# Normalised input of token blocks 2 to 8: half-precision pairs kept in DRAM and read back transposed by DMA, in place of transpositions on TensorE

## The chip, the cores and the metric

The kernel runs on one core of a Trainium2 chip. Its engines, each with its own in-order queue of instructions, are TensorE (PE in the profile, with PEld for its weight loads), VectorE (DVE), ScalarE (ACT), GpSimd (POOL) and SyncE (SP); SP and GpSimd also issue DMAs. The metric is the device time of one launch in microseconds, smaller being better; where several runs are given it is their median.

## The reference

A two-layer decoder trunk on 2048 tokens of width 1024: a Mamba-2 mixer, then multi-head latent attention (MLA), each behind an RMS norm with gain, with residual adds.

```python
def rms_norm(x, g):
    y = xf * lax.rsqrt(jnp.mean(xf * xf, axis=-1, keepdims=True) + EPS)
    return y * g
# layer 1: Mamba-2
hn = rms_norm(x, g_pre[0])
proj = hn @ w_in                      # gate z, conv input xBC, dt: 1024 -> 5152
xBC = silu(causal_depthwise_conv(xBC, conv_w, conv_b))
y = ssd_chunked_scan(xh, softplus(dt + bias), A, B, C) + D_skip * xh
h = x + group_norm(y * silu(z)) * g_out @ w_out
# layer 2: MLA
ckv, k_rope = split(rms_norm(h, kv_g_in) @ w_dkv);  k_nope, v = rms_norm(ckv) @ w_ukv
cq, gate = split(rms_norm(h, g_pre[1]) @ w_in);     q = rms_norm(cq) @ w_uq
h = h + (causal_attention(q, k, v) * silu(gate)) @ w_out
out = rms_norm(h, g_final)
```

The result has single precision. The kernel gets near it with half-precision products by splitting every factor into a pair, `hi` (rounded to half precision) and `lo` (the remainder), and adding three products, hi*hi + hi*lo + lo*hi.

## The kernel before

**Blocks.** The tokens are worked in blocks of 512 (`TB`). There are eight of them in the sense of this document: blocks 1 to 4 are the four quarters of the sequence as input of the Mamba layer, blocks 5 to 8 the same quarters of `h` as input of the MLA layer's projections. (In the code they are `xT[0]` to `xT[7]`.) After them come attention and the output projection, which the change doesn't touch.

**The input of a block.** Every product with the normalised input needs it with channels on the partitions: eight tiles `xT` of [128 channels, 2 halves of the pair, 512 tokens] in half precision, in eight buffers that the next block takes over one by one. `load_x` loads four tiles of 128 rows by 1024 channels (`hx`; for one block `hs`), squares them on ScalarE, makes reciprocal roots on VectorE (`rows_rms`, `rsqrt`: 12 small operations) and scales the rows (line 574). `prep` then makes the eight tiles: for each of eight groups of 128 channels four transpositions on TensorE into one PSUM bank (`transposed`, line 262), and from there the pair (`pair16`): ScalarE writes `hi` (line 115), VectorE the remainder `lo` (line 116). In the Mamba layer the pair's scale is the gain `g0` of the channel, in the MLA layer a constant, since the MLA weights hold their gain.

**Mamba.** The work runs over 16 items (block, group of heads). While the state scan `ssd` of an item is done in 20 pieces, the queue of TensorE gets beside it the output projection `outp` of the item before, and the input products `xbc` and the gate's `zgate` of the next item. `sweep` orders the products of these: channel groups 0 and 1 for all four banks, then 2 to 5 group by group, then 6 and 7 bank by bank. In the third item of a block, `load_x` of the next block is called, and `prep` is spread under the last `zgate` of the block, which is the last user of the old `xT`. Behind it stands `steps` (step sizes dt of the next block, 16 products with `wdt`, line 729), which needs all eight new tiles.

**Weights.** In block 1 the weights come raw (`wraw`, or held tiles), are split in `wpair` into pairs (`wsp`) with the scale `up` of their kind, and are kept in DRAM (`wi_d`, written by `settle`); later blocks load them from there. `scan` and `powers` find these scales. The output weights are handled likewise in blocks 1 and 2 (`w_out`, `wo_d`). Weight loads are written with a raised priority.

**MLA.** For each of four blocks: `load_x` of the next block, `mla_kv_down` and `mla_cq` (products with one `xT` tile after another), the upper projections `mla_up` beside the gate's products `mla_gate`, and under the second half of `mla_gate` (the last user of `xT`) the `prep` of the next block.

**Order.** Nothing is placed by hand: a scheduler puts the instructions on the engines' queues by their priority and a model of their times, and gives each its waits. Nearly all DMAs are issued on SP's one queue, where a DMA that waits holds up those behind it.

Of the kernel before, what the change touches and what calls it, by code (L numbers as in the profile page):

```python
# [12 lines left out]
BF16 = mybir.dt.bfloat16  # L13
# [54 lines left out]
class Net:  # L68
# [93 lines left out]
    def scan(self, g, kinds, place, hold=False, early=0):  # L162
# [40 lines left out]
    def wpair(self, b, kind, g, k, w):  # L203
# [4 lines left out]
        with self.tc.high_priority(AHEAD):  # L208
            u = self.t(self.wp, "wsp", [P, 2, 2, n], F16, bufs=WSP)
            d = self.wi_d[kind][g, k // 2]  # L210
            if b == 0:
# [9 lines left out]
                for j, raw in enumerate(raws):  # L221
                    self.pair16(u[:, j, 0], u[:, j, 1], raw, self.up[:, g, kind:kind + 1])
# [54 lines left out]
    def layer_constants(self, cp):  # L277
# [14 lines left out]
        self.up, self.down = (cp.tile([P, G, 3], F32, name=n) for n in ("up", "down"))  # L292
        self.half = cp.tile([P, G], F32, name="half")
# [19 lines left out]
        nc.vector.tensor_scalar(self.g0, self.g0, up[:, 0:1], 1.0 / 32, ALU.mult, ALU.mult)  # L313
        self.pair16(self.wdt[:, :, 0], self.wdt[:, :, 1], wdt.rearrange("p (k c) -> p k c", k=KD), up[:, 1:2])
# [21 lines left out]
    def mamba(self, cp):  # L336
# [32 lines left out]
        for part in (hold, self.prep(0, self.g0), rest[0], self.steps(0), together(self.xbc(0, 0), rest[1]),  # L369
# [10 lines left out]
        for n, (b, g) in enumerate(items):  # L380
# [4 lines left out]
            turned = iter(())  # L385
            if g == G - 2:
                self.load_x(b + 1, self.a["x"][(b + 1) * TB:(b + 2) * TB] if b + 1 < NB else self.h_d[0:TB])
                turned = behind(self.prep(b + 1, self.g0 if b + 1 < NB else None, each=1), 2)
            if n + 1 < len(items):
# [7 lines left out]
                parts += [beneath(self.xbc(*items[n + 1]), beside), beneath(self.zgate(*items[n + 1]), beside, turned)]  # L397
# [162 lines left out]
    def load_x(self, b, src, tag="hx"):  # L560

        nc = self.nc
        self.xn[b] = xs = [self.t(self.hh, tag, [P, D], bufs=4) for _ in range(4)]
# [3 lines left out]
        parts = 4 if b == 0 else 1  # L567
        for c in range(parts):
            for i, x in enumerate(xs):
                v = x[:, c * D // parts:(c + 1) * D // parts]  # L570
                if parts > 1 and i == 3:
# [4 lines left out]
    def prep(self, b, gain=None, tag="tr", each=4):  # L576
# [3 lines left out]
        for k in range(KD):  # L580
            ps = self.transposed(xs, k, tag)
            u = self.t(self.xq, "xT", [P, 2, TB], F16, bufs=8)
            self.pair16(u[:, 0, :], u[:, 1, :], ps, XSCALE if gain is None else gain[:, k:k + 1])
            self.xT[b].append(u)
            if k % each == each - 1:
                yield

# [343 lines left out]
    def mla(self, early):  # L931
# [5 lines left out]
        for b in range(NB):  # L937
            last = b == NB - 1
            if not last:
# [705 lines left out]
```

## Time and profile before

| | |
|---|---|
| runs | 2917.16 us median of 3 (2916.06 to 2920.21) |
| profiled execution | 2911.01 us, span 2909.2 us |
| mean granted TensorE clock | 0.993 |
| block boundaries in the Mamba layer (`steps` begins) | 356.6, 723.1, 1088.0 us |
| Mamba layer and MLA projections end about | 2000 us |
| ScalarE, GpSimd busy | 1828.1 us (63%), 860.4 us (30%) |
| DMA | 441.40 MB, 152 GB/s mean |

"Busy" counts the time in which an engine has an instruction in work; products on TensorE overlap, so the distance between two starts, and not the length of one, is what it costs. In the grouped views a row has the code line, engine, operation, output <- input (buffer numbers left out), shape, count, and then busy time, mean ns of one, idle time before the group and what ended it. In a timeline the columns are start, length, engine, line, operation, names, count, and in brackets the idle time before it.

### The profile page before, as it was taken

The numbers are of one execution on the slowest core, as the hardware profiler recorded it, in microseconds if no ns is written. First come the engines' busy times: TensorE is split into PE (matmuls) and PEld (weight loads), VectorE is DVE, ScalarE is ACT, GpSimd is POOL, SyncE is SP. The second block draws the span as 40 slices with busy tenths as digits, with TensorE's granted clock in tenths as the row PEclk, the third lists the DMA queues.
The fourth block names the chain that finished last, engine by engine and source line by source line (L and its number), as shares of the span: only waits on it lengthen the run. The fifth ranks groups of instructions, "written<-read, shape, count | busy, mean of one in ns | idle before, by whom it ended". The sixth has DMA issues, their size and how long they took to land.

```text
span 2909.2 us, 58684 instructions
## 1 busy us (share of the span) xinstructions
PE 2833.6 (97%) x21582; PEld 1668.1 (57%) x21582; DVE 2109.2 (73%) x5068; ACT 1828.1 (63%) x3976; POOL 860.4 (30%) x984
## 2 busy tenths in 40 slices
PE   7899999999999999999999999999999999999998
PEld 3465566555555554554555545555666666665787
DVE  6789887787777778779775554456777777778454
ACT  8777756666566766556553433334888888888522
POOL 0222221221221212222211121213665666665300
PEclk9999999999999999999999999999999999999999
DMA  8755536444464446635445655662212222222453
GB/s 286 256 191 190 177 121 207 150 144 153 160 233 132 152 136 229 220 118 192 157 147 204 206 183 176 204 196 81 67 52 67 67 53 72 64 67 88 169 194 109
DMA packets 244899, 441.40 MB, mean 152 GB/s; under 512 B 69890, under 2 KB 111650, under 8 KB 243172
## 3 DMA queue, kind: packets, MB, share of 16 engines
q1 hardware_dynamic: 233476, 401.74, 43.0%
q0 software_dynamic: 11136, 35.92, 3.4%
q8 instruction: 169, 2.77, 0.4%
q14 instruction: 118, 0.97, 0.1%
HBM read 332.83 MB, written 104.73 MB: 150 GB/s over the span
## 4 chain that ended last, share of the span: by engine, by line
PE 43%; issue 3%; DVE 3%; ACT 2%; DMA 1%; POOL 1%; DVEq 0%; SPq 0%; POOLq 0%; ACTq 0%
PE s L1326 4%; PE s L1327 4%; PE mm L84 4%; PE s L1328 4%; PE mm L86 4%; PE mm L85 4%; PE s L1213 4%; PE tr L84 3%; PE tr L86 3%; PE tr L85 3%; PE o L1366 2%; PE o L1367 2%; PE o L1365 2%; DVE junk L1215 1%; PE s L1394 0%
## 5 line engine op out<-in xcount | busy, mean ns | idle before, releaser
L1350 POOL TENSOR_TENSOR PTs<-x,PTs 128x512 f16<-128x512 f32 (+1 forms) x380 | 439.0, 1178 | 263.5 <-ACT PTs L1337 174.5
L1332 ACT ACTIVATE x<-s 128x512 f32<-128x512 f32 (+3 forms) x640 | 326.7, 524 | 50.3 <-PE s L1328 31.6
L84 PE MATMUL mm<-xT,wsp 128*128 128x512 f16 x800 | 306.6, 383 | 7.9 <-ACT wsp L115 5.6
L85 PE MATMUL mm<-xT,wsp 128*128 128x512 f16 x800 | 306.1, 383 | 0.0
L86 PE MATMUL mm<-xT,wsp 128*128 128x512 f16 x800 | 305.3, 382 | 0.0
L1337 ACT ACTIVATE PTs<-x 128x1024 f16<-128x1024 f32 (+1 forms) x320 | 297.2, 929 | 9.4
L1215 DVE CUSTOM_DVE_ANT_0 junk<-s,fence,mx 128x512 bf16<-128x512 f32 (+1 forms) x372 | 242.1, 651 | 43.7 <-PE s L1213 3.0
L1367 PE MATMUL o<-K,PTs 128*128 128x65 f16 x2176 | 262.2, 192 | 2.0 <-POOL PTs L1350 1.5
L1365 PE MATMUL o<-K,PTs 128*128 128x64 f16 x2176 | 263.4, 192 | 0.0
L1366 PE MATMUL o<-K,PTs 128*128 128x65 f16 x2176 | 263.3, 194 | 0.0
L802 POOL TENSOR_TENSOR Xp<-Xw,Xp 128x512 fp32r<-128x512 f32 x64 | 89.5, 1399 | 500.3 <-ACT Xp L801 299.8
L85 PE MATMUL mm<-wsp,xT 128*128 128x512 f16 (+1 forms) x640 | 231.5, 362 | 3.2 <-DVE wsp L116 3.2
L84 PE MATMUL mm<-wsp,xT 128*128 128x512 f16 (+1 forms) x640 | 231.4, 362 | 3.2 <-ACT craw L606 2.9
L1365 PEld LDWEIGHTS <-PTs 128*128 128x128 f16 x2176 | 204.5, 97 | 51.6 <-issue 3.6
L612 DVE SCALAR_TENSOR_TENSOR cacc<-craw,pack,cacc 128x512 f32<-128x512 f32 x288 | 215.5, 777 | 23.9 <-ACT cacc L610 22.9
L1366 PEld LDWEIGHTS <-PTs 128*128 128x128 f16 x2176 | 202.4, 97 | 53.0 <-issue 0.3
L86 PE MATMUL mm<-wsp,xT 128*128 128x512 f16 (+1 forms) x640 | 231.6, 362 | 0.0
L1326 PE MATMUL s<-xT,K 98*128 98x512 f16 (+1 forms) x628 | 218.5, 348 | 4.1 <-DVE mx L1215 3.7
L1213 PE MATMUL s<-K,xT 96*128 96x512 f16 (+1 forms) x616 | 213.9, 350 | 5.6 <-DVE mx L1215 4.1
L1327 PE MATMUL s<-xT,K 96*128 96x512 f16 (+1 forms) x628 | 218.4, 348 | 0.0
L1328 PE MATMUL s<-xT,K 96*128 96x512 f16 (+1 forms) x628 | 217.0, 345 | 0.0
L1367 PEld LDWEIGHTS <-PTs 128*128 128x128 f16 x2176 | 201.4, 98 | 2.7 <-POOL PTs L1350 1.8
(477 smaller groups left out, 7243.4 us busy)
## 6 DMA issues: line engine op xcount, KB each, us to landing
wsp<-wi_d SPq DMA_DIRECT2D x96, 512.0 KB
big<-cumT SPq DMA_DIRECT2D x64, 512.0 KB
wraw<-in_ssm_w_out_dram SPq DMA_DIRECT2D x96, 256.0 KB
wi_d<-wsp SPq DMA_DIRECT2D x32, 512.0 KB
wsp<-wo_d SPq DMA_DIRECT2D x32, 512.0 KB
wsp<-wu_d SPq DMA_DIRECT2D x28, 512.0 KB
hx<-in_ssm_w_in_dram SPq DMA_DIRECT2D x48, 256.0 KB
wraw<-in_ssm_w_in_dram SPq DMA_DIRECT2D x48, 256.0 KB
```

Source lines behind the costliest of these rows:

```text
L84: mm(out, l_hi, r_hi, start=start, stop=False)
L85: mm(out, l_hi, r_lo, start=False, stop=False)
L86: mm(out, l_lo, r_hi, start=False, stop=stop)
L1213: self.nc.tensor.matmul(s[:, :w], Q[0:96], K[0:96], start=True, stop=True)
L1326: mm(s, K[0:98, 0, ks], Q[0:98, 0, c], start=True, stop=False)
L1327: mm(s, K[0:96, 0, ks], Q[0:96, 1, c], start=False, stop=False)
L1328: mm(s, K[0:96, 1, ks], Q[0:96, 0, c], start=False, stop=kb < 4 * qb)
L1332: act(o, s, AF.Exp)
L1350: engine.tensor_tensor(u[:, 1, a:b], x[:, a:b], u[:, 0, a:b], ALU.subtract)
L1365: mm(o[:, 0:64], hi, V[:, k, 0:64], start=k == 0 and j == 0, stop=False, skip_group_check=True)
L1366: mm(o[:, 0:65], hi, V[:, k, 64:129], start=False, stop=False, skip_group_check=True)
L1367: mm(o[:, 0:65], lo, V[:, k, 64:129], start=False, stop=k == 4 * qb + j, skip_group_check=True)
```

## The change

For blocks 2 to 8 the input is no longer transposed on TensorE. A new `rows_in` handles a block in two halves of 256 rows: two `hx` tiles are loaded, squared, and their reciprocal roots multiplied by a constant (`rx`); then the pair is made with the rows on the partitions, 128 x 1024 at once, into two further `hx` buffers in the order channel group, half of the pair, channel, and stored to a DRAM tensor `xp_d` of [512, 2048] in half precision. `fill` makes the eight `xT` tiles with one transposing DMA each, of 512 rows by 256 columns of `xp_d`. `rows_in` stands under `outp` and `xbc` of the Mamba items, or between the parts of an MLA block; `fill` stands where `prep` stood. `load_x` and `prep` remain for block 1 alone.

Since the rows are now scaled before the transposition, the Mamba layer's gain `g0` can't be applied per channel there. It moves into the weights: `scan` makes `gu`, the product of `g0` and `up`, for each weight group, `wpair` splits with it, and the weights `wdt` of the step sizes are multiplied by `g0` once.

```diff
@@ scan
+        for kind in kinds:
+            nc.vector.tensor_scalar(self.gu[:, g % 2, kind], self.g0, self.up[:, g, kind:kind + 1], None, ALU.mult)
@@ wpair
-                    self.pair16(u[:, j, 0], u[:, j, 1], raw, self.up[:, g, kind:kind + 1])
+                    self.pair16(u[:, j, 0], u[:, j, 1], raw, self.gu[:, g % 2, kind, k + j:k + j + 1])
@@ layer_constants
-        nc.vector.tensor_scalar(self.g0, self.g0, up[:, 0:1], 1.0 / 32, ALU.mult, ALU.mult)
-        self.pair16(self.wdt[:, :, 0], self.wdt[:, :, 1], wdt.rearrange("p (k c) -> p k c", k=KD), up[:, 1:2])
+        nc.vector.tensor_scalar(self.g0, self.g0, up[:, 0:1], 2.0 ** -15, ALU.mult, ALU.mult)
+        wdt = wdt.rearrange("p (k c) -> p k c", k=KD)
+        nc.vector.tensor_tensor(wdt, wdt, self.g0.unsqueeze(2).to_broadcast([P, KD, H]), ALU.mult)
+        self.pair16(self.wdt[:, :, 0], self.wdt[:, :, 1], wdt, up[:, 1:2])
@@ mamba
             if g == G - 2:
-                self.load_x(b + 1, self.a["x"][(b + 1) * TB:(b + 2) * TB] if b + 1 < NB else self.h_d[0:TB])
-                turned = behind(self.prep(b + 1, self.g0 if b + 1 < NB else None, each=1), 2)
+                fresh = thinned(self.rows_in(b + 1, self.a["x"][(b + 1) * TB:(b + 2) * TB] if b + 1 < NB
+                                             else self.h_d[0:TB]), 1)
+                parts[-1] = beneath(parts[-1], fresh)
+                turned = behind(self.fill(b + 1), 2)
...
-                parts += [beneath(self.xbc(*items[n + 1]), beside), beneath(self.zgate(*items[n + 1]), beside, turned)]
+                parts += [beneath(self.xbc(*items[n + 1]), beside, fresh),
+                          beneath(self.zgate(*items[n + 1]), beside, turned)]
@@ new
+    def rows_in(self, b, src, tag="hx"):
+        nc = self.nc
+        for at in (0, 2 * P):
+            xs = [self.t(self.hh, tag, [P, D], bufs=4) for _ in range(2)]
+            for i, x in enumerate(xs):
+                nc.sync.dma_start(x, src[at + i * P:at + (i + 1) * P, :])
+            yield
+            r = self.rows_rms(xs, [self.t(self.sp, "yt", [P, D], BF16, bufs=2) for _ in xs], D)
+            up = self.t(self.sm, "rx", [P, 2], bufs=2)
+            nc.vector.tensor_scalar(up, r, XSCALE, None, ALU.mult)
+            us = [self.t(self.hh, tag, [P, KD, 2, P], F16, bufs=4) for _ in range(2)]
+            for i, (x, u) in enumerate(zip(xs, us)):
+                self.pair16(u[:, :, 0], u[:, :, 1], x.rearrange("p (k c) -> p k c", k=KD), up[:, i:i + 1])
+            yield
+            for i, u in enumerate(us):
+                nc.sync.dma_start(self.xp_d[b][at + i * P:at + (i + 1) * P, :], u.rearrange("p k n c -> p (k n c)"))
+
+    def fill(self, b):
+        self.xT[b] = []
+        for k in range(KD):
+            u = self.t(self.xq, "xT", [P, 2, TB], F16, bufs=8)
+            self.nc.sync.dma_start_transpose(u, self.xp_d[b][:, k * 2 * P:(k + 1) * 2 * P])
+            self.xT[b].append(u)
+            yield
@@ mla
-                self.load_x(NB + b + 1, self.h_d[(b + 1) * TB:(b + 2) * TB], "hs" if b == 1 else "hx")
+            fresh = ... self.rows_in(NB + b + 1, self.h_d[(b + 1) * TB:(b + 2) * TB], "hs" if b == 1 else "hx")
+            go(fresh, 1)          # and again behind mla_kv_down, mla_cq, and in the loop over mla_gate(b, 0)
...
-            after = self.first_maxima() if last else self.prep(NB + b + 1, None, "mm", 1)
+            after = self.first_maxima() if last else self.fill(NB + b + 1)
```

What this does to the queues is shown at three places. The first is TensorE at the end of block 1, from the last product of the last `zgate` (`mm` from `xT` and `wsp`) to the first product of `steps` (`wdt`); `y` is the output of the scan that is turned, `Xp` and `Bt` belong to the state. Before:

```order
L86 MATMUL mm_3719<-wsp_3941,xT_318 128x512
L262 MATMUL tr_3995<-pack,hx_2945 128x128
L262 MATMUL tr_3995<-pack,hx_2946 128x128
L262 MATMUL tr_3995<-pack,hx_2947 128x128
L262 MATMUL tr_3995<-pack,hx_2948 128x128
L84 MATMUL tr_4003<-Xp_3824,Bt_3747 128x512
L85 MATMUL tr_4003<-Xp_3824,Bt_3747 128x512
L86 MATMUL tr_4003<-Xp_3824,Bt_3747 128x512
```

and, behind eight more transpositions,

```order
L84 MATMUL mm_4128<-wsp_4135,yT_3318 128x512
L808 MATMUL tr_4025<-pack,y_3815 128x128 x4
L85 MATMUL mm_4128<-wsp_4135,yT_3318 128x512
L729 LDWEIGHTS wdt
L729 MATMUL tr_4033<-xT_3804,wdt 64x512
```

After:

```order
L86 MATMUL mm_3782<-wsp_3980,xT_329 128x512
L84 MATMUL tr_4030<-Xp_3881,Bt_3810 128x512
L85 MATMUL tr_4030<-Xp_3881,Bt_3810 128x512
L86 MATMUL tr_4030<-Xp_3881,Bt_3810 128x512
L843 MATMUL tr_4040<-pack,y_3872 128x128 x4
L764 LDWEIGHTS wdt
L764 MATMUL tr_4048<-xT_3862,wdt 64x512
```

The transpositions of `hx` are gone, and `steps` follows the gate's last product by three state products and four turns.

The second place is SP's queue at the end of block 2, during the last `zgate`; `wraw` here are raw output weights, `wo_d` the stores of their pairs. Before:

```order
L226 DMA wsp_8029<-wi_d 128x2048
L683 DMA wraw_8379<-in_ssm_w_out_dram 128x512
L200 DMA wo_d<-wsp_8214 128x2048
L683 DMA wraw_8422<-in_ssm_w_out_dram 128x512
L683 DMA wraw_8423<-in_ssm_w_out_dram 128x512
L200 DMA wo_d<-wsp_8303 128x2048
```

After:

```order
L228 DMA wsp_8061<-wi_d 128x2048
L619 DMA_TRANSPOSE xT_7947<-xp_d 128x2x512
L619 DMA_TRANSPOSE xT_7989<-xp_d 128x2x512
L619 DMA_TRANSPOSE xT_8005<-xp_d 128x2x512
L619 DMA_TRANSPOSE xT_8059<-xp_d 128x2x512
L619 DMA_TRANSPOSE xT_8081<-xp_d 128x2x512
L718 DMA wraw_8387<-in_ssm_w_out_dram 128x512
L202 DMA wo_d<-wsp_8222 128x2048
L718 DMA wraw_8430<-in_ssm_w_out_dram 128x512
L619 DMA_TRANSPOSE xT_8101<-xp_d 128x2x512
```

Five transposing DMAs stand ahead of the raw load `wraw_8387`, a sixth behind the next load; the last two follow four rows further.

The third place is ScalarE's queue at the same point; the split of `wraw_8387` into `wsp`, the gate's evictions `sz`, the turned `y` (`yT`), and the eviction of `steps` (`yt` with `dtdown`). Before, from the last eviction of the gate on:

```order
L635 ACTIVATE sz_8072<-mm_7809,half 128x512
L115 ACTIVATE xT_8080<-tr_8075,pack 128x512
L115 ACTIVATE xT_8095<-tr_8090,pack 128x512
L115 ACTIVATE xT_8103<-tr_8098,pack 128x512
L115 ACTIVATE yT_8111<-tr_8106 128x512
L733 ACTIVATE yt_8132<-tr_8114,dtdown 64x512
```

After, from the split on:

```order
L115 ACTIVATE wsp_8385<-wraw_8387,gou 128x512
L836 ACTIVATE Ct_8461<-BC_7588 128x128
L670 ACTIVATE sz_8069<-mm_7862,half 128x512
L920 ACTIVATE yt_8041,ms_7082<-y_7957 128x512
L115 ACTIVATE wsp_8429<-wraw_8430,gou 128x512
L670 ACTIVATE sz_8078<-mm_7863,half 128x512
```

The evictions of `xT` are gone; the split that needs the load behind the five DMAs stands ahead of the gate's evictions.

More of the change, by code (lines that the diff above doesn't have):

```diff
@@ L368, in mamba @@
         ahead = self.scan(1, (0, 1, 2), later)
-        for part in (hold, self.prep(0, self.g0), rest[0], self.steps(0), together(self.xbc(0, 0), rest[1]),
+        for part in (hold, self.prep(0), rest[0], self.steps(0), together(self.xbc(0, 0), rest[1]),
                      together(self.zgate(0, 0), ahead)):
@@ L558, in second_powers, with load_x @@
         yield
-    def load_x(self, b, src, tag="hx"):
+    def load_x(self, b, src):
         nc = self.nc
-        self.xn[b] = xs = [self.t(self.hh, tag, [P, D], bufs=4) for _ in range(4)]
+        self.xn[b] = xs = [self.t(self.hh, "hx", [P, D], bufs=4) for _ in range(4)]
         for i in range(4):
@@ L566, in load_x @@
         r = self.rows_rms(xs, [self.t(self.sp, "yt", [P, D], BF16, bufs=2) for _ in xs], D)
-        parts = 4 if b == 0 else 1
-        for c in range(parts):
+        for c in range(4):
             for i, x in enumerate(xs):
-                v = x[:, c * D // parts:(c + 1) * D // parts]
-                if parts > 1 and i == 3:
+                v = x[:, c * D // 4:(c + 1) * D // 4]
+                if i == 3:
                     nc.scalar.activation(v, v, AF.Copy, scale=r[:, i:i + 1])
@@ L574, in load_x, with prep @@
                     nc.vector.tensor_scalar(v, v, r[:, i:i + 1], None, ALU.mult)
-    def prep(self, b, gain=None, tag="tr", each=4):
+    def prep(self, b):
         xs = self.xn.pop(b)
@@ L580, in prep @@
         for k in range(KD):
-            ps = self.transposed(xs, k, tag)
+            ps = self.transposed(xs, k)
             u = self.t(self.xq, "xT", [P, 2, TB], F16, bufs=8)
-            self.pair16(u[:, 0, :], u[:, 1, :], ps, XSCALE if gain is None else gain[:, k:k + 1])
+            self.pair16(u[:, 0, :], u[:, 1, :], ps, XSCALE)
             self.xT[b].append(u)
-            if k % each == each - 1:
+            if k % 4 == 3:
                 yield
+    def rows_in(self, b, src, tag="hx"):
[21 more added lines that the diff above has]
+            yield
     def xbc(self, b, g):
@@ L938, in mla @@
             last = b == NB - 1
-            if not last:
-                self.load_x(NB + b + 1, self.h_d[(b + 1) * TB:(b + 2) * TB], "hs" if b == 1 else "hx")
+            fresh = iter(()) if last else self.rows_in(NB + b + 1, self.h_d[(b + 1) * TB:(b + 2) * TB],
+                                                       "hs" if b == 1 else "hx")
+            go(fresh, 1)
             tables = self.rope_tables(b)
@@ L944, in mla @@
             go(kv, 1)
+            go(fresh, 1)
             cq = self.mla_cq(b)
             go(cq, 1)
+            go(fresh, 1)
             go(kv)
+            go(fresh, 1)
             self.qT = []
@@ L955, in mla @@
                 go(up, 3 if last else 2)
+                go(fresh, 1)
                 if n == 2 and b:
@@ L1572, in run @@
             self.o_d = dp.tile([D, T], F32, name="o_d")
+            self.xp_d = [dp.tile([TB, 2 * D], F16, name=f"xp{b}_d") for b in range(2 * NB)]
             self.m_d = dp.tile([NH * NB, P, 32], F16, name="m_d")
```

4 lines of the change are left out of this document (3 added, 1 removed).

## The prediction

> **What bounds the kernel now.** I read the engines' busy times first, then the same table by stage, to see whether one engine is the limit in the stages that the change touches.
>
> ```profile
> PE 2833.6 (97%) x21582; PEld 1668.1 (57%) x21582; DVE 2109.2 (73%) x5068; ACT 1828.1 (63%) x3976; POOL 860.4 (30%) x984
> ```
> ```profile
> core 0: us, PE busy (x) PEld busy (x) DVE busy (x) ACT busy (x) POOL busy (x), PEclk, DMA share, GB/s
> 360.00:620.00 260.00, 258.85 (x1565) 151.00 (x1565) 206.51 (x455) 155.31 (x412) 59.47 (x71) 1.00 0.45 153
> 620.00:850.00 230.00, 224.73 (x1343) 118.19 (x1342) 180.51 (x437) 144.49 (x377) 40.75 (x52) 1.00 0.51 169
> 1600.00:1720.00 120.00, 119.19 (x648) 63.86 (x646) 67.00 (x151) 51.91 (x96) 23.46 (x38) 1.00 0.61 202
> ```
>
> TensorE is busy for 98 to 99.6% of these stages; the first two rows are Mamba blocks 2 and 3, the last is one of the attention blocks' projections. VectorE has 21 to 22% of slack beside it in the Mamba stages and 44% in the last. An instruction taken off TensorE's queue should therefore shorten the span by the time until its successor starts.
>
> **The change, part by part.** *Transpositions removed.* Seven blocks lose 8 groups of 4. The view of line 262 has 336 such instructions; 80 of them turn latents (`tr<-pack,xs`) and 32 of the `hx` rows belong to block 1, so 160 - 32 + 64 + 32 = 224 go.
>
> ```profile
> L262 PE MATMUL tr<-pack,hx x160: 272/273/455, 17.2 to 1462.5; 128*128 128x128 f32 x160
> L262 PE MATMUL tr<-pack,xs x80: 272/273/329, 1546.7 to 1928.7; 128*128 128x128 f32 x80
> L262 PE MATMUL mm<-pack,hx x64: 272/273/273, 1597.7 to 1874.8; 128*128 128x128 f32 x64
> L262 PE MATMUL mm<-pack,hs x32: 272/273/273, 1718.2 to 1755.3; 128*128 128x128 f32 x32
> ```
>
> One lasts 273 ns, but they are pipelined. What a group costs is the distance of starts in TensorE's timeline:
>
> ```profile
> 1604.38 0.38 PE L86 MATMUL mm<-yT,wsp 128*128 128x512 f16 x1
> 1604.59 0.60 PE L262 MATMUL mm<-pack,hx 128*128 128x128 f32 x4
> 1605.03 0.38 PE L84 MATMUL tr<-xT,st 128*128 128x512 f16 x1
> ```
>
> That is 1605.03 - 1604.59 = 0.44 us, and 56 groups give **-24.6 us**.
>
> *Waits that go with them.* At the block boundaries TensorE also waits for VectorE to evict the turned tiles from PSUM:
>
> ```profile
> PE tr L808 <- DVE xT L116: 1.4, 3, 0.9
> PE tr L879 <- DVE xT L116: 0.7, 1, 0.7
> ```
>
> These evictions no longer exist, so **-2.1 us**. (What is late next there is the DMA, below.)
>
> *Work on VectorE and ScalarE.*
>
> ```profile
> L116 DVE SCALAR_TENSOR_TENSOR xT<-tr,pack,xT 128x512 f16<-128x512 f32 x24 | 17.5, 743 | 8.7 <-ACT xT L115 8.7
> L116 DVE SCALAR_TENSOR_TENSOR xT<-mm,xT 128x512 f16<-128x512 f32 x24 | 16.4, 682 | 0.0
> L116 DVE SCALAR_TENSOR_TENSOR xT<-tr,xT 128x512 f16<-128x512 f32 x8 | 5.2, 683 | 2.8 <-ACT xT L115 2.8
> L574 DVE TENSOR_SCALAR hx<-hx,rsy 128x1024 f32<-128x1024 f32 x24 | 16.5, 749 | 0.2
> L245 DVE SCALAR_TENSOR_TENSOR rsy<-rsq,rsy 128x4 f32<-128x4 f32 x81 | 12.8, 158 | 1.7
> L1503 DVE SCALAR_TENSOR_TENSOR h<-h,rsy,gf 128x1024 f32<-128x1024 f32 x12 | 14.6, 1280 | 0.1
> L115 ACT ACTIVATE xT<-tr,pack 128x512 f16<-128x512 f32 x24 | 16.4, 714 | 2.8 <-PE tr L262 2.8
> L115 ACT ACTIVATE xT<-mm 128x512 f16<-128x512 f32 x24 | 14.1, 587 | 7.1 <-PE mm L262 7.1
> L115 ACT ACTIVATE xT<-tr 128x512 f16<-128x512 f32 x8 | 4.5, 640 | 0.0
> L1337 ACT ACTIVATE PTs<-x 128x1024 f16<-128x1024 f32 x192 | 203.0, 1057 | 5.9
> ```
>
> VectorE loses 39.1 us of evictions and 28 row scalings of 0.75 us (21 us). It gains 28 half-precision remainders of 128x1024, taken at the 1.28 us of the same operation on that shape (35.8 us), and a second reciprocal-root chain per block with two scalings: 7 x 14 operations of 0.16 us, 15.7 us. Together about -9 us. ScalarE loses 35.0 us and gains 28 x 1.06 = 29.6 us. Neither comes nearer to being the bound; I take **0**. If the neighbouring rows mislead (0.75 or 1.5 us for a remainder), it is -15 to +6 us spread over 1,700 us in which VectorE is idle a quarter of the time.
>
> *Block 1 and the weights.* The gain moves into a pointer that the weight splits read anyway; new are three scalings of 8 columns for each group of weights (at 0.16 us) and one product of 128x256. All but the first of them stand where VectorE has room. Only in the first 60 us, before TensorE is fed, can they lie on the path: **+0.5 us**, between 0 and 1.5.
>
> *Traffic.* Each block writes 2.1 MB to `xp_d` and reads it back, 29.4 MB for seven.
>
> ```profile
> q1 hardware_dynamic: 233476, 401.74, 43.0%
> ```
>
> 401.74 MB in 43.0% of 2909.2 us is 321 GB/s while the engines are busy; at that rate 29.4 MB are 92 us of all 16 engines, spread over about 1,700 us: the share in the tables rises from about 0.53 to 0.58. Taken as hidden, since TensorE loses only 0.4 to 2.3% in the rows with shares of 0.45 to 0.61. If it is not hidden, it is part of the slow case below.
>
> *The transpositions that read back, the open term.* `fill` issues eight per block on SP, each of 256 KB, and each waits until TensorE has read the old `xT` tile for the last time. No row of the trace shows such a DMA. Where it decides is the boundary between two Mamba blocks, where `steps` needs all eight tiles right after the last product of the gate:
>
> ```profile
> 718.99 0.60 PE L262 MATMUL tr<-pack,hx 128*128 128x128 f32 x4
> 719.35 0.48 PE L84 MATMUL tr<-Xp,Bt 128*128 128x512 f32 x1
> 720.12 1.04 PE L262 MATMUL tr<-pack,hx 128*128 128x128 f32 x8
> 722.51 0.65 PE L808 MATMUL tr<-pack,y 128*128 128x128 f32 x4 [0.92 <-DVE xT L116]
> 723.10 3.63 PE L729 MATMUL tr<-xT,wdt 128*64 128x512 f16 x16
> ```
>
> Call the end of the gate's last product T0 (718.99 here). By the new order three state products (0.77 us with their start), four turns of `y` (0.44) and then `steps` follow, 16 products at 3.63/16 = 0.227 us. The last tile, freed at T0 itself, is needed at T0 + 0.77 + 0.44 + 14 x 0.227 = T0 + 4.4 us. What the nearest rows say of a DMA:
>
> ```profile
> gate_d<-xs POOLq DMA_DIRECT2D x24, 256.0 KB, 3.0
> v_d<-Xp POOLq DMA_DIRECT2D x8, 256.0 KB, 4.3
> L1231 SPq DMA_DIRECT2D xT<-m_d x124: 602/650/835, 2004.8 to 2694.9; - x124
> 1592.51 9.63 DMA hs<-h_d
> ```
>
> 256 KB land 3.0 to 4.3 us after the issue (medians on another queue), SP needs up to 0.65 us to issue one, and the tile before is 0.8 us of transfer (256 KB at 321 GB/s). So the last lands at T0 + 0.65 + 0.8 + 4.3 = 5.75 us, 1.35 us late; with 3.0 us it is not late; with the 9.6 us that 512 KB of `h_d` took in the chain behind other loads it is 0.65 + 9.6 - 4.4 = 5.9 us late. I take 1.35 us, the value by the rows of this size, at three boundaries: **+4.0 us** (0 to 17.7). At the fourth boundary a whole output projection of 96 products stands between. In the attention blocks the first user takes one tile after another:
>
> ```profile
> 1638.73 0.29 PE L84 MATMUL mm<-wsp,xT 128*128 128x288 f16 x1
> 1640.20 0.54 PE L84 MATMUL mm<-wsp,xT 128*128 128x288 f16 x2
> ```
>
> The 12 products of one tile take 1.47 us, so the eighth tile has 7 x 1.47 = 10.3 us. I charge nothing there.
>
> Queued behind these waits on SP are the raw loads of the next output weights (the rows in the change's section). The load of `wraw_8387` stands behind five transpositions, and ScalarE's split of it stands ahead of the gate's evictions. Behind the fifth tile's last reading 36 of the gate's products still lie before T0, 0.21 us each by the starts above, 7.7 us, so a load of 0.65 + 4.3 us is still in time.
>
> Two rules of the Trainium skill speak to the open term, against each other. "Advanced Engine Details and Errata", section "X-Bar Transpose (TRN2)", says that these DMAs run as fast as regular ones; that would be the 4.0 us above or less. "VectorE: DVE Perf Modes", section "The three transpose paths", gives 1309 ns to a DMA transposition of 128x128 in two-byte data, against 390 ns on TensorE. Of the second figure the trace differs: 273 ns each and 0.11 us apart. Of the first no run here shows anything. If the eight such squares of one DMA went one by one, an estimate from that page is 10.5 us each, which makes the time about 3,220 us by the working of the third rival.
>
> **The sum.** The profiled execution took 2911.0 us (span 2909.2). 2911.0 - 24.6 - 2.1 + 0.5 + 4.0 = 2888.8 us. The runs' median, 2917.2, lies 6.2 us above that execution, so I forecast **2895 us**.
>
> **Rivals.** *1. Late landings.* The read-back takes as long as the slowest 512 KB load, 5.9 us late at three boundaries: 2911.0 - 26.7 + 0.5 + 17.7 = 2902.5, as a median 2909 us. For it: SP's queue and the rings are shared with weight loads. Against it: that load followed right behind the store of the same rows.
>
> *2. TensorE is not the bound in the Mamba stages.* The longest pieces of the chain of waits there lie on VectorE and ScalarE, such as this one:
>
> ```profile
> 1413.90 2.65 DVE cacc L612 x4
> ```
>
> Then 32 groups (14.1 us) would only turn into waiting, and the 24 of the attention blocks remain: 2911.0 - 10.6 + 0.5, as a median 2907 us. Against it: TensorE idles 1.2 of 260 us in the quiet Mamba stage.
>
> *3. The transposing DMA is slow: the case that ends slower.* If the data move in packets of 256 bytes (one row of one 128-column half), a DMA of 512 rows by 256 columns is 1,024 packets. A packet of q1 took 0.430 x 16 x 2909.2 us / 233476 = 86 ns of one engine, which is 5.5 us per DMA over 16 engines, 44 us for eight. The first tiles are free 19 us before T0 (the group behind the third tile's 12 products starts at 700.26: 718.99 - 700.26 + 2.6, less five groups that go), so the last lands at T0 - 19 + 44 + 3 = T0 + 28, 23.6 us late, three times 71 us. In the attention blocks a step is 5.0 us (the groups at 1604.59 and 1609.56), the first tiles are free six steps, 30 us, before the end, and the last is 44 - 30 + 3 - 10.3 = 6.7 us late, three times 20 us. In all 2911.0 - 26.2 + 91 = 2976, as a median 2982 us.
>
> ```profile
> 700.26 0.60 PE L262 MATMUL tr<-pack,hx 128*128 128x128 f32 x4
> ...
> 1609.56 0.60 PE L262 MATMUL mm<-pack,hx 128*128 128x128 f32 x4
> ```
>
> The point from which it decides: 3 x (8t - 20.4) = 26.2, t = 3.6 us per DMA. For it: the packets, and that a transposition scatters each row over 128 partitions. Against it: the mean packet carries 1.7 KB, so a short one should take less than 86 ns. It is the only place where a loss of this size can come from.
>
> *4. Nothing moves:* a median of 2917 us, if the change's gain and delays of 8 to 9 us at each Mamba boundary cancel.
>
> **How the numbers follow.** The forecast gets 0.55, late landings 0.12, the chain 0.08, nothing 0.05, the slow DMA 0.20. A measurement of this kernel tells about 0.2% from no change, 5.8 us, so "same" is 2911 to 2923 us. Forecast, the chain and half of the late landings are faster, 0.68 with a little taken off for what I have not seen; same 0.12; slower 0.20. The range begins at 2886 us (no late tile, -4, and the spread of the runs, -4) and reaches to 2940 us, into the slow case up to a DMA of about 4.4 us. Above it are most of the slow case, 0.15, and little is below.
>
> **What would show it.** 21358 matmuls instead of 21582, and 112 transpositions on the helper's line, confirm the removal. In the timeline of TensorE at the three Mamba boundaries, `steps` waits for `xT<-xp_d` by 0 to 2 us if the forecast holds, by 6 if the first rival does, by over 20 if the third does; then ScalarE's splits of output weights also wait for loads, and the DMA share at the boundaries rises well over 0.6. If TensorE idles more in the middle of the blocks by as much as it lost in work, it is the second. Wrong would be the forecast too if the new row work, now in two halves, blocks ScalarE ahead of an eviction that TensorE waits for: waits of TensorE for `craw` or `wsp` that were not there.

## The result, and the profile after

The changed kernel took 2895.24 us (median of 4 runs, 2890.99 to 2896.14) against 2916.61 us before (4 runs): ratio 0.9926, 95% interval 0.9911 to 0.9941. Two more sets of five runs gave 0.9935 (0.9922 to 0.9949) and 0.9931 (0.9918 to 0.9943), so the change is worth about 0.7%, 20 us. The profiled executions differ by less, 2911.01 to 2894.94 us, since the one of before lies under the median of its runs; ratios are used below.

First the engines' busy times of the changed kernel, then the stages that the prediction read (columns: us, then busy time of TensorE, its weight loads, VectorE, ScalarE, GpSimd; granted clock, DMA share, GB/s), then the line of the turning helper and the new DMAs.

```profile
PE 2809.5 (97%) x21358; PEld 1643.2 (57%) x21358; DVE 2105.2 (73%) x5123; ACT 1826.1 (63%) x3948; POOL 854.8 (30%) x984
```
```profile
360.00:620.00 260.00, 257.44 (x1559) 148.07 (x1558) 207.25 (x460) 158.05 (x418) 56.01 (x71) 1.00 0.45 150
620.00:850.00 230.00, 221.85 (x1341) 115.98 (x1340) 180.01 (x430) 141.18 (x371) 42.15 (x53) 1.00 0.59 192
1600.00:1720.00 120.00, 119.25 (x630) 61.62 (x629) 60.00 (x135) 48.80 (x85) 24.79 (x40) 1.00 0.75 235
```
```profile
L264 PE MATMUL tr<-pack,xs x80: 272/273/330, 1537.1 to 1911.6; 128*128 128x128 f32 x80
L264 PE MATMUL tr<-pack,hx x32: 272/421/454, 17.2 to 22.8; 128*128 128x128 f32 x32
...
L619 SPq DMA_TRANSPOSE xT<-xp_d x56: 1223/1252/3721, 331.0 to 1856.8; - x56
```
```profile
DMA packets 308068, 470.77 MB, mean 163 GB/s; under 512 B 129474, under 2 KB 171234, under 8 KB 306340
...
q1 hardware_dynamic: 296644, 431.11, 47.7%
```

All 224 transpositions are gone and 24.1 us of TensorE's busy time with them. VectorE and ScalarE are as busy as before. The granted clock, 0.993 before and 0.994 after, is not what changed. 63,168 more packets went through q1. SP spends 1.25 us on each transposing DMA, twice what the prediction allowed. The second stage idles 3 us more than before: TensorE now waits there. The waits of TensorE around the boundary of blocks 2 and 3 (690 to 760 us), in the order engine, waiting line, releaser, us in all, times, longest:

```profile
PE tr L843 <- ACT y L942: 2.4, 1, 2.4
PE tr L804 <- DVE big L802: 1.2, 1, 1.2
PE tr L85 <- POOL Xp L837: 0.7, 1, 0.7
PE tr L764 <- DMA xT<-xp_d: 0.5, 2, 0.3
```

In TensorE's timeline of the same boundary, with the wait in brackets:

```profile
715.78 0.66 PE L843 MATMUL tr<-pack,y 128*128 128x128 f32 x4 [2.42 <-ACT y L942]
716.37 2.78 PE L764 MATMUL tr<-xT,wdt 128*64 128x512 f16 x12
719.38 0.59 PE L764 MATMUL tr<-xT,wdt 128*64 128x512 f16 x2 [0.24 <-DMA xT<-xp_d]
720.25 0.59 PE L764 MATMUL tr<-xT,wdt 128*64 128x512 f16 x2 [0.27 <-DMA xT<-xp_d]
```

TensorE waits for the last two tiles, by 0.5 us and not by 1.35, and only here. In front of them stands something that the prediction did not have: the turns of `y` now wait 2.42 us (0.92 before), so the tiles gain that much time. They need it. The gate's last product in TensorE's timeline, and SP's timeline behind it:

```profile
712.29 0.38 PE L86 MATMUL mm<-wsp,xT 128*128 128x512 f16 x1
```
```profile
714.18 0.33 SPq L202 DMA_DIRECT2D wo_d<-wsp  x1
714.60 3.53 SPq L619 DMA_TRANSPOSE xT<-xp_d  x2
```

The gate's last product ends at about 712.5 us (0.21 us after its start, the distance of starts), and TensorE gets the last tile at 720.25, 7.7 us later, where the prediction had 5.75. SP issues the last two DMAs only behind a store of `wo_d`.

### The profile page after: what moved, and what is told of

It is laid out like the page before. It is cut to its first block, busy times and chain, and to the rows that moved or that the text cites. A ratio compares the mean times of both kernels' runs of the same rounds, so it can differ in the third digit from the quotient of the medians.

```text
span 2893.2 us, 58394 instructions
## 1 busy us (share of the span) xinstructions
PE 2809.5 (97%) x21358; PEld 1643.2 (57%) x21358; DVE 2105.2 (73%) x5123; ACT 1826.1 (63%) x3948; POOL 854.8 (30%) x984
## 4 chain that ended last, share of the span: by engine, by line
PE 68%; DVE 16%; DMA 6%; ACT 5%; issue 4%; SPq 1%; POOL 1%; DVEq 0%; ACTq 0%; POOLq 0%
PE mm L84 11%; PE mm L85 11%; PE mm L86 11%; PE s L1365 4%; PE s L1366 4%; PE s L1367 4%; PE s L1252 4%; PE tr L85 3%; PE tr L84 3%; PE tr L86 3%; DVE cacc L647 3%; PE o L1405 2%; PE o L1406 2%; PE o L1404 2%; DMA big<-cumT 2%
## 5 line engine op out<-in xcount | busy, mean ns | idle before, releaser
L1404 PEld LDWEIGHTS <-PTs 128*128 128x128 f16 x2176 | 204.6, 97 | 52.1 <-issue 4.3
L1405 PEld LDWEIGHTS <-PTs 128*128 128x128 f16 x2176 | 202.7, 97 | 53.4 <-issue 1.0
L84 PE MATMUL mm<-wsp,yT 128*128 128x512 f16 (+1 forms) x512 | 197.8, 386 | 7.9 <-DVE sz L671 6.3
```

The costliest lines, as they stand in the source:

```text
L84: mm(out, l_hi, r_hi, start=start, stop=False)
L1404: mm(o[:, 0:64], hi, V[:, k, 0:64], start=k == 0 and j == 0, stop=False, skip_group_check=True)
L1405: mm(o[:, 0:65], hi, V[:, k, 64:129], start=False, stop=False, skip_group_check=True)
```

## The experiments

Twelve kernels, each against the kernel before on the same chip, five rounds each. First the change in parts. `c1_changed` and `c3_changed` are the changed kernel itself.

> The changed kernel once more, beside the kernel before on the same chip, as the yardstick for the parts. Medians of the first runs differ by 21.4 us (2916.6 to 2895.2), the two profiled executions by 16.1 us. Theory 1 (TensorE's 56 groups of transpositions come off at 0.44 us each, 24.6 us, with 2.1 us of its waits for the xT evictions, and part of this is given back as new waits of TensorE for evictions and for y in the Mamba stages): 17 to 21 us faster. Theory 2 (what is given back is lost to contention of the 63,168 added DMA packets and to transposing DMAs that block SP's queue): the same total, so this run does not tell 1 from 2. Theory 3 (nothing is given back, the profiled execution of before was a fast one): 24 to 27 us faster.

Measured: 2898.16 us, 0.9935 (0.9922 to 0.9949), 18.9 us faster (14.9 to 22.7). That is the yardstick; it fits theory 1 or 2, not 3.

`c1_weights` keeps the old `load_x` and `prep` (with the constant scale) for all blocks:

```diff
-                fresh = thinned(self.rows_in(b + 1, ...), 1)
-                turned = behind(self.fill(b + 1), 2)
+                self.load_x(b + 1, ...)
+                turned = behind(self.prep(b + 1, each=1), 2)
...
-            after = self.first_maxima() if last else self.fill(NB + b + 1)
+            after = self.first_maxima() if last else self.prep(NB + b + 1, "mm", 1)
```

> Only the first norm's factors moved into the weights; all eight blocks are scaled, transposed on TensorE and split as before. Theories 1 to 3 agree: 56 small VectorE products more and none of TensorE's work gone, so the kernel before within 1.5 us either way (the prediction's term was +0.5 us). If it alone is more than 3 us faster or slower, the parts below cannot be read as the stores and transposing DMAs alone.

Measured: 2915.38 us, 1.0003 (0.9994 to 1.0011). The gain in the weights costs nothing that can be told from zero (1.7 us faster to 3.2 slower).

`c1_mamba_part` has the new path in the Mamba loop alone: of that diff it keeps the last two lines (with `load_x` for `rows_in` in `mla`). `c1_mla_part` has it in `mla` alone, and keeps the lines of the Mamba loop.

> The gain in the weights, and the new path for token blocks 2 to 5 only (their rows are prepared during the Mamba part, 32 transposing DMAs); blocks 6 to 8 are transposed on TensorE as before. Theory 1: 32 groups x 0.44 = 14.1 us and 2.1 us of waits come off, and nearly all of the 8.1 us of new TensorE idle time is in this part: 6 to 10 us faster than before. Theory 2 (contention and SP): the DMA engines are busiest in the MLA part (share up to 0.77 there, 0.56 here), so little is lost here: 12 to 16 us faster. Theory 3: 15 to 17 us faster.

Measured: 2906.14 us, 0.9965 (0.9952 to 0.9977), 10.2 us faster.

> The gain in the weights, and the new path for token blocks 6 to 8 only (24 transposing DMAs in the MLA part); blocks 2 to 5 are transposed on TensorE as before. Theory 1: TensorE is 98.5 to 100% busy in these stages in both traces, so all of 24 x 0.44 = 10.6 us is kept: 9 to 12 us faster than before. Theory 2: the loss sits here, where the DMA share rises from 0.56 to 0.77: 2 to 7 us faster. Theory 3: 10 to 11 us faster. The two parts together should give the whole change within 2 us if they do not act on one another.

Measured: 2905.88 us, 0.9969 (0.9956 to 0.9981), 9.0 us faster. The parts add up to the whole (19.2 and 18.9 us). The Mamba part lies at the upper end of theory 1, but its interval, 6.7 to 14.0 us, reaches into theory 2, and the MLA part's, 5.5 to 12.8 us, tells nothing apart. The traces tell more, since whole executions also differ by what follows the last stretch below (1000 to 1004 us, whatever the kernel). So I measured stretches: from the first start of `steps` in one block to that in the next, and in the MLA part from one block's rotary product on VectorE (`cacc<-tr,sz`, 16 partitions) to the next one's. One profiled execution each, three of the changed kernel:

| kernel | block 1 | block 2 | block 3 | MLA 1 | MLA 2 | MLA 3 |
|---|---|---|---|---|---|---|
| before | 329.0 | 366.5 | 364.9 | 119.6 | 120.5 | 119.6 |
| c1_weights | 327.8 | 367.8 | 365.1 | 119.6 | 120.5 | 119.6 |
| c1_mamba_part | 326.8 | 365.8 | 362.6 | 119.6 | 120.5 | 119.6 |
| c1_mla_part | 328.8 | 368.0 | 364.2 | 117.5 | 117.2 | 117.1 |
| changed (3) | 321.8 to 325.9 | 366.0 to 366.8 | 362.5 to 363.3 | 117.0 to 117.8 | 117.2 | 117.2 |
| c2_turns_back | 328.2 | 366.3 | 365.7 | 120.8 | 120.6 | 120.6 |
| c2_plain_loads | 323.2 | 366.7 | 361.9 | 116.9 | 117.2 | 117.2 |
| c2_two_issues | 324.8 | 368.2 | 364.8 | 117.1 | 117.2 | 117.1 |
| c2_pool_halves | 324.8 | 372.7 | 368.2 | 116.9 | 117.2 | 117.2 |
| c3_one_rows | 326.5 | 363.5 | 362.4 | 116.1 | 116.1 | 116.1 |
| c3_no_low | 324.9 | 364.8 | 361.9 | 117.1 | 117.2 | 117.1 |
| c4_rows_moved | 330.6 | 370.3 | 362.6 | 126.7 | 116.1 | 116.1 |

Eight groups of 0.44 us are 3.5 us a stretch. Block 1 got 3.1 to 7.2 us (it varies most from one execution to the next) and the second MLA stretch 3.3; block 2 got next to nothing, block 3 about 2 us, the other MLA stretches 2 to 2.5 us. Between the last Mamba column and the first MLA column lies block 4 with the start of the MLA part, from the third start of `steps` to the first rotary product: 460.2 us before, 457.4 to 462.1 in the changed kernel.

*Is it lost cover?* `c2_turns_back` gives TensorE its work back, unread:

```diff
             self.xT[b].append(u)
+            self.transposed([self.pack] * 4, 0, "tr" if b <= NB else "mm")
             yield
```

> The changed kernel, and at each of the 56 fill steps four transpositions of the constant tile on TensorE into a bank that nobody reads: TensorE gets the removed work back, while its evictions by ScalarE and VectorE stay away and the rows, stores and transposing DMAs stay. Theory 1 (the removed work had covered TensorE's waits for y, for the evictions of the gate and of Xp): 24 us of work come back, but some 6 of the 8 us of new idle time go, so 15 to 20 us slower than the changed kernel, and that is level with the kernel before to 4 us faster than it; TensorE's wait for y (L942) at the second boundary, 2.4 us in the changed kernel, falls under 1 us. Theory 2 (what was given back is DMA contention and SP's queue): it stays given back, so all 24 us come on top: 24 us slower than the changed kernel, and 3 to 7 us slower than the kernel before.

Measured: 2918.43 us, 1.0015 (1.0006 to 1.0024): 23.3 us slower than the changed kernel (1.0015 - 0.9935; 24.5 and 25.9 us by its two other ratios) and 4.4 us slower than before. These are the numbers of theory 2, and theory 1 is out as the general cause. The three MLA stretches grew by 3.0 to 3.8 us, eight groups' worth, and keep their waits for `Xp` and `big`. Only in block 2 do the turns cost nothing, as theory 1 has it, and there the wait for `y` is gone from the list of the boundary:

```profile
PE tr L805 <- DVE big L803: 1.3, 1, 1.3
PE tr L765 <- DMA xT<-xp_d: 1.3, 2, 1.1
PE tr L85 <- POOL Xp L838: 0.7, 1, 0.7
```

*Is it the transposing DMAs?* `c2_plain_loads`:

```diff
-            self.nc.sync.dma_start_transpose(u, self.xp_d[b][:, k * 2 * P:(k + 1) * 2 * P])
+            self.nc.sync.dma_start(u, self.xp_d[b][k * 64:(k + 1) * 64, :].rearrange(...))
```

> The changed kernel with each transposing DMA made a plain DMA of the same 256 KB and into the same tile, so the tiles hold rows and not their transposition (the transposition is left out). 1,024 packets of 256 bytes per DMA become 128 of 2 KB, and SP's issue falls from 1.25 us to about 0.35 us. Theory 1: the transposing DMAs have slack, so within 2 us of the changed kernel (17 to 21 us faster than before). Theory 2: contention and SP's queue cost 5 to 8 us, which come back: 23 to 28 us faster than before. Rival 3 of the prediction (slow transposing DMAs), if something of it is left: TensorE's waits for wsp from wo_d and wi_d and for xT go, 1 to 3 us.

Measured: 2892.32 us, 0.9931 (0.9915 to 0.9948), as the changed kernel, and its stretches lie within 0.6 us of that kernel's. Theory 2 is out as far as the transposition goes. Its queue row prices one:

```profile
q1 hardware_dynamic: 245572, 431.10, 45.6%
```

The share of 16 engines' span is 0.477 x 16 x 2893.2 = 22081 us in the changed kernel and 0.456 x 16 x 2890.6 = 21090 here, so a transposing DMA takes 991/56 = 17.7 us of one engine more than a plain one of the same bytes, 1.1 us over 16. (This is the time of packets, which overlap: the share in `c4_rows_moved` reaches 1.20 from 1620 to 1630 us.) The third rival had 5.5 us for the whole DMA, 4.7 above the plain one's 0.8.

`c2_two_issues` splits each of these DMAs in two halves:

```diff
-            self.nc.sync.dma_start_transpose(u, self.xp_d[b][:, k * 2 * P:(k + 1) * 2 * P])
+            for n in range(2):
+                self.nc.sync.dma_start_transpose(u[:, n, :], self.xp_d[b][:, (2 * k + n) * P:(2 * k + n + 1) * P])
```

> The changed kernel with two transposing DMAs of 128 KB for each tile in place of one of 256 KB: the same packets, twice the issues on SP (56 more at about 1.25 us if the issue is a fixed price, 0 us more in all if it goes by size). It tells how much slack SP's queue and the last tile of a boundary have. Theory 1: the last tile lands later by at most one issue, 1.25 us, which comes behind TensorE's wait for y at the second boundary: 0 to 3 us slower than the changed kernel, with the wait of steps for xT rising from 0.5 to at most 4 us. Theory 2 (SP's queue is what costs): 56 more blockings, 4 to 8 us slower.

Measured: 2903.19 us, 0.9966 (0.9955 to 0.9978), 9 to 11 us slower than the changed kernel, above what theory 1 allowed and just over theory 2's 8 us. The view of the line (times in ns) shows that SP's price does not go by size:

```profile
L620 SPq DMA_TRANSPOSE xT<-xp_d x112: 1122/1251/2082, 333.2 to 1865.0; - x112
```

`steps` waits 3.4 us for `xT<-xp_d` (0.5 before the split), and blocks 2 and 3 are 1.4 and 1.5 us over the changed kernel's longest. The rest stays open: this profiled execution, 2899.1 us, was the fastest of its runs. So two issues per tile cost time, while at one there is slack: the plain loads, at 0.32 us an issue, gained nothing.

`c2_pool_halves` was meant to free VectorE at the second boundary, by a product and a difference on GpSimd for every second piece of the output weights in block 2:

```diff
+                    nc.gpsimd.tensor_scalar(raws[i], raws[i], s, None, ALU.mult)
+                    nc.scalar.activation(u[:, i, 0], raws[i], AF.Copy)
+                    nc.gpsimd.tensor_tensor(u[:, i, 1], raws[i], u[:, i, 0], ALU.subtract)
```

> The changed kernel, and in block 2 every second piece of the output weights has its low half made by GpSimd (a product and a difference) in place of VectorE: 32 instructions of 0.74 us leave VectorE's queue, among them some of those that stand between the steps of y at the second boundary. Theory 1 with its cause in VectorE's queue: the wait for y (L942) at the second boundary falls from 2.4 us to 0.5 to 1.5 us, and the time by 1 to 3 us, if the pieces do not come late. Rival (the chain of y's own instructions is the limit, not the queue): the wait stays at 2 to 2.4 us and the time is the same. It can lose as well: GpSimd's products of 512 columns last 1.2 to 1.5 us, and TensorE may wait for wsp.

Measured: 2908.83 us, 0.998 (0.9972 to 0.9989), 13 us slower than the changed kernel; there were 16 such pieces, not 32. The wait for `y` stayed at 2.5 us, and TensorE's waits for the gate's `sz` rose from 4.5 to 10.8 us (300 to 1500 us). VectorE's and GpSimd's timelines of this run at the boundary:

```profile
717.29 1.64 DVE L923 TENSOR_TENSOR y<-y,yt 128x512 f32<-128x512 f32 x1
718.85 1.17 DVE L116 SCALAR_TENSOR_TENSOR wsp<-wraw,gou,wsp 128x512 f16<-128x512 f32 x1
```
```profile
716.78 1.60 POOL L727 TENSOR_TENSOR wsp<-wraw,wsp 128x512 f16<-128x512 f32 x1
718.36 2.00 POOL L725 TENSOR_SCALAR wraw<-wraw,gou 128x512 f32<-128x512 f32 x1
```

While GpSimd works, these two instructions of VectorE, 0.94 and 0.74 us in the changed kernel, take 1.64 and 1.17. Three others beside GpSimd, which take one input from PSUM (`tr`), keep their 0.67 to 0.68 us. So the run did not free VectorE there and says nothing on the cause.

`c3_no_low` frees VectorE without GpSimd:

```diff
-    self.pair16(u[:, i, 0], u[:, i, 1], raws[i], self.gou[...])
+    nc.scalar.activation(u[:, i, 0], raws[i], AF.Copy, scale=self.gou[...])
+    nc.vector.memset(u[:, i, 1], 0.0)
```

> The changed kernel, and in block 2 the low halves of the output weights are set to zero on VectorE in place of being worked out (that part of the computation is left out): 32 instructions of 0.75 us become memsets, which should be under half as long, so the four that stand between the steps of y at the second boundary nearly go. If VectorE's queue is what TensorE waits for there (theory 1 in block 2, where putting the turns back cost nothing: 366.3 us against 366.7 us): the wait for y (L942) of 2.4 us falls to 1.2 us or less, and the stretch from the second to the third start of steps from 366.7 to 364 to 366 us; 1 to 3 us in all. Rival (y's own chain with its passes between VectorE and ScalarE is the limit): the wait stays above 2 us and the stretch at 366.7 us.

Measured: the wait for `y` at the boundary fell to 1.2 us and block 2 to 364.8 us, as the first theory has it. In the total, 2891.81 us and 0.9925 (0.9913 to 0.9938), it cannot be told from the changed kernel. There are 32 memsets of 0.27 us. So at that boundary VectorE's queue, with output weights between the steps of `y`, is one thing that sets the end, and part of TensorE's 3.5 us there only becomes waiting; the next run shows another part.

*Is it the row work?* `c3_one_rows`:

```diff
         nc = self.nc
+        if b > 1:
+            return
...
-            self.nc.sync.dma_start_transpose(u, self.xp_d[b][:, k * 2 * P:(k + 1) * 2 * P])
+            self.nc.sync.dma_start_transpose(u, self.xp_d[1][:, k * 2 * P:(k + 1) * 2 * P])
```

> The changed kernel, but only token block 2 has its rows loaded, scaled, split and stored; blocks 3 to 8 read block 2's rows back (so the input of those blocks is left out), with all 56 transposing DMAs as they were. Gone are 24 row tiles' instructions on VectorE and ScalarE (1.28 and 1.14 us each, with the squares) and their loads and stores; on TensorE nothing changes. Theory 4, formed after the second set (putting TensorE's turns back cost all 23 us, so in the MLA part its waits were not cover lost: the waits for Xp and big, 0.75 us a block, stand behind row work in VectorE's queue): the stretches between the MLA blocks' rotary products fall from 117.1 to 116.3 us, and blocks 2 and 3 of the Mamba part by up to 1 us each, in all 2 to 5 us faster than the changed kernel (0.9914 to 0.992 of before). Theory 1 (the waits are evictions that the removed turns had covered): the stretches stay at 117.1 us and the time within 1 us of the changed kernel.

> The changed kernel once more, as the yardstick of this set: 0.9926 and 0.9935 of before so far, so 0.992 to 0.995 here. In its stretches: 323 to 326, 366.5 to 367, 362 to 363.5 us for the first three blocks and 117.0 to 117.8 us for the MLA blocks; what varies besides is the attention part, 907 to 910 us, whose clock is not 1.00.

Measured: 2888.32 us, 0.9911 (0.9898 to 0.9925), beside 2894.09 us and 0.9931 for the changed kernel: 5.8 us between the medians, though the intervals overlap. The stretches are sharper. In block 2, 363.5 us, 2.5 to 3.3 us went, more than the 1 us that was expected, with the wait for `y` still at 2.4. What is gone there is a wait for `big`, which the kernel before does not have in that block. In the changed kernel TensorE's wait, and VectorE's timeline:

```profile
PE tr L914 <- DVE big L883: 1.4, 1, 1.4
```
```profile
650.41 2.48 DVE L116 SCALAR_TENSOR_TENSOR hx<-hx,rx,hx 128x1024 f16<-128x1024 f32 x2 [0.56 <-ACT hx L115]
654.46 1.22 DVE L883 TENSOR_TENSOR big<-big,CB 128x1024 f32<-128x1024 f32 x1
```

Two remainders of rows, 2.48 us, stand ahead of `big` in that queue, with four instructions between. In the MLA part the view by windows (us, TensorE busy, clock, DMA share, GB/s) gives, first for the changed kernel, then for this one:

```profile
1538.66:1656.46 117.80, 116.22 (x618) 1.00 0.79 251
1656.46:1773.61 117.15, 116.40 (x618) 1.00 0.74 226
1773.61:1890.76 117.15, 116.40 (x618) 1.00 0.72 224
```
```profile
1533.06:1649.12 116.06, 116.06 (x618) 1.00 0.70 217
1649.12:1765.20 116.08, 116.08 (x618) 1.00 0.66 203
1765.20:1881.27 116.07, 116.07 (x618) 1.00 0.68 206
```

Without row work TensorE does not wait in these stretches, and 119.55 - 116.06 = 3.5 us is what eight groups are worth. With it, the waits of TensorE from 1500 to 1900 us in the changed kernel are:

```profile
PE mm L84 <- DMA wsp<-wo_d: 1.6, 1, 1.6
PE tr L264 <- DVE Xp L116: 0.9, 2, 0.5
PE tr L84 <- DVE big L116: 0.6, 2, 0.3
```

VectorE's timeline of the changed kernel shows how the row work makes the second and third:

```profile
1672.15 0.15 DVE L247 SCALAR_TENSOR_TENSOR rsy<-rsq,rsy 128x2 f32<-128x2 f32 x1
1672.26 0.69 DVE L1033 SCALAR_TENSOR_TENSOR sz<-sz 128x512 f32<-128x512 f32 x1
1672.87 0.16 DVE L606 TENSOR_SCALAR rx<-rsy 128x2 f32<-128x2 f32 x1
1672.94 0.74 DVE L116 SCALAR_TENSOR_TENSOR Xp<-tr,mdown,Xp 128x512 f16<-128x512 f32 x1
1674.94 2.48 DVE L116 SCALAR_TENSOR_TENSOR hs<-hs,rx,hs 128x1024 f16<-128x1024 f32 x2 [1.25 <-ACT hs L115]
1677.34 0.74 DVE L116 SCALAR_TENSOR_TENSOR big<-tr,mdown,big 128x512 f16<-128x512 f32 x1
```

TensorE waits 0.46 and 0.28 us for the remainders of `Xp` and `big`. That of `Xp` stands in VectorE's queue behind the rows' chain of roots (L243 to L247, 0.15 us a link) and their scaling `rx`; that of `big` behind 1.25 us in which VectorE waits for ScalarE's `hs` and two remainders of rows, 2.48 us. The wait for `wsp<-wo_d` comes by SP. Its queue's longest wait from 1535 to 1590 us, and its timeline:

```profile
SPq L612 <- DVE hx L116: 12.6, 2, 11.8
```
```profile
1559.12 1.53 SPq L612 DMA_DIRECT2D xp_d<-hx  x2
1560.74 0.41 SPq L725 DMA_DIRECT2D wsp<-wo_d  x1
```

SP stands 11.8 us in front of the store of the new rows, which waits for VectorE's remainders, and the weight load behind it goes out late. `c1_changed` and `c3_changed` have the same: SP stands 11.4 us, and TensorE waits 0.8 and 1.3 us. The first MLA stretch is longer by as much, 117.0, 117.5 and 117.8 us with waits of 0.8, 1.3 and 1.6.

By stretches, block 2 and the MLA part lost 5.6 to 7.2 us to the row work. Block 4 with the start of the MLA part is shorter without it too, 453.9 us, by 3.5 to 8.2. But there the kernel before waits as well (3.6 us for `sz` and `hs`), and `c3_one_rows` also leaves out the loads, squares and roots which that kernel had. So its 5.8 us are the price of all the row work of six blocks, not only of what the change added.

`c3_one_rows` took the arithmetic away together with loads and stores. `c4_rows_moved` puts those back:

```diff
+            if b > 1:
+                yield
+                for i, x in enumerate(xs):
+                    nc.sync.dma_start(self.xr_d[b][at + i * P:at + (i + 1) * P, :], x)
+                continue
             r = self.rows_rms(xs, ...)
```

> It parts the two things that c3_one_rows took away together. Blocks 3 to 8 have their rows loaded and stored again (the same number of DMAs and bytes, the rows stored as they came), but none of the row arithmetic: no squares, no scaling and no splitting on ScalarE and VectorE, and fill still reads block 2's rows (so the input of those blocks is left out). If the row arithmetic is what cost the 5 to 6 us (theory 4), this run is like c3_one_rows: 0.990 to 0.992 of before, and 116.1 us between the MLA blocks. If it was the loads and stores and what they do to SP's queue and the DMA engines (theory 2 in a new place), it is like the changed kernel: 0.9925 to 0.9945 and 117.1 us.

Measured: 2908.79 us, 0.998 (0.9969 to 0.999), 14 us slower than the changed kernel, which neither theory expected. Two of the three MLA stretches are 116.1 us, so there the loads and stores cost nothing and the arithmetic was the price. In block 2 the wait for `big` is gone as well, and block 4 with the start of the MLA part takes 455.2 us, so there too the arithmetic is the likelier price; but block 2 as a whole is longer, 370.3 us, since `steps` waits 4.1 us for `xT`. The first MLA stretch is 126.7 us, by one wait of TensorE, with SP's (1600 to 1652 us) behind it:

```profile
PE mm L84 <- DMA wsp<-wd_d: 7.7, 1, 7.7
```
```profile
SPq L607 <- DMA hx<-h_d: 11.5, 3, 9.0
```
```profile
1639.44 0.32 SPq L607 DMA_DIRECT2D xr_d<-hx  x1
1644.71 0.43 SPq L124 DMA_DIRECT2D wsp<-wd_d  x1
```

The bare stores come early in SP's queue, stand there waiting for their own loads (9.0 us before the one at 1639.44), and hold up the weights. The stretch grew by 10.6 us and not by 7.7, since TensorE's clock is halved behind the wait, as the view by windows has it:

```profile
1649.80:1654.80 5.00, 4.99 (x21) 0.50 0.71 209
1656.00:1672.60 16.60, 16.60 (x109) 1.00 0.47 144
```

So this kernel's total does not answer the question for the Mamba part; it shows what a wait at the head of SP's queue can cost.

No kernel here that computes the whole output beats the changed one. Why block 3 got 2 us and not 3.5 stays open. Another order of the row work on VectorE in `mla`, or stores that wait on another queue, were not tried.

## Why the prediction was right

Its sum went from 2911.0 to 2888.8, 22.2 us, and the runs show about 20. The mechanism held: work came off TensorE and was worth its time there. Two terms were mis-sized, in opposite directions.

- *Transpositions, -24.6:* right. Putting them back costs 23 to 26 us, and 3.0 to 3.8 us in each MLA stretch. Block 2 is the exception: there the second rival (VectorE's chain as the bound) holds locally.
- *Waits for `xT` evictions, -2.1:* they are gone. The turns of `y` beside them wait longer instead (5.3 us in all between 300 and 1900 us, 0.5 before). The sum has no term for this.
- *Block 1 and the weights, +0.5:* 0.9 us by `c1_weights`, interval -1.7 to +3.2.
- *The read-back, +4.0:* too large; 0.5 us measured (0 to 0.7 in the three executions). That is luck in part. The last tile came later than reckoned, 7.7 us behind the gate at the second boundary and not 5.75, and SP's issue takes 1.25 us, not 0.65; but TensorE comes to `steps` later, behind `y`. The transposition itself adds 1.1 us over the 16 engines per DMA. By the third rival's own point, 3.6 us per DMA, it was not slow enough to decide. The Trainium skill, "Advanced Engine Details and Errata", section "X-Bar Transpose (TRN2)", says that transposing DMAs are as fast as regular ones. The equal time of the plain-load run does not show that, since both kinds are hidden there; in packet time the transposing one took 17.7 us of one engine more.
- *Work on VectorE and ScalarE, 0:* the step that failed. The busy times were nearly right, VectorE -4.0 us and ScalarE -2.0 us in all (about -9 and -5.4 in the prediction), and the inference from them was not: what counts is where the instructions stand. The evictions that went were of 0.7 us; the new remainders are of 1.28 us, two at a time, ahead of evictions and stores that others wait for. Without the row work the gain rises by 5.8 us, to 25.9 us (0.9911; 21.9 to 29.7). That this is the arithmetic is shown for two MLA stretches; in block 2 the lost wait for `big` points to it, and for the rest of the Mamba part it stays open.
- *Traffic, 0:* right in the MLA stretches: the DMA share rose to 0.79, and the one DMA that TensorE waited for was a load that stood late in SP's queue.
- *The 6.2 us from the profiled execution to the median* was a chance of that execution: in the later sets the median of before lay 3 to 4 us above it (2914.2 to 2915.4 us). The changed kernel's profiled execution lies at its median, 2894.9 and 2895.2 us. That the forecast met the time to the microsecond is therefore partly luck: profile against profile, the sum was 6.1 us too low.

With 0.5 us for the read-back and 5.8 for the row work, and the other terms as predicted, the sum is 24.6 + 2.1 - 0.5 - 0.5 - 5.8 = 19.9 us. That it meets the 20 proves little: the 5.8 is uncertain by several us and holds row work that the kernel before had too. Of its own signs of error, "waits of TensorE for `craw` or `wsp`", the one for `wsp` came (0.8 to 1.6 us), through SP's store rather than through ScalarE.

## What to carry to other kernels

In this kernel, work moved off the bounding engine was worth its full time only where nothing else was about to end last: look at each boundary, not at the mean share. Work that an idle-looking engine takes over is not free by its busy time: see which eviction, store or load stands behind each new instruction, the longest first. A store on the queue that also loads weights holds those weights until its data are ready.

## What the hardware showed that I had not expected

SP needs 1.25 us to issue a transposing DMA of 256 KB, and the same for 128 KB; a plain store of 512 KB takes it 0.34 us. The read-back moves in packets under 512 bytes, 59,584 more of them for 56 DMAs, 1,064 each, and each DMA's packets take 1.1 us of all 16 engines more than the plain load's. Two of VectorE's passes over 128x512 slowed from 0.74 and 0.94 us to 1.17 and 1.64 beside a GpSimd instruction that works on the same shape, while passes with one input from PSUM did not slow. And a wait of TensorE can cost more than its length: behind one of 7.7 us its clock was 0.50 for 5 us, and the stretch grew by 10.6.
